# Output projection of a two-branch decoder layer by Strassen's scheme: 28 weight products of 512 columns in place of 32 per pair of blocks

## The chip, the cores and the metric

The kernel runs on one core of a Trainium2 chip. The metric is device time in microseconds (us), lower is better.

## The reference

One layer, on 4096 rows of 1024 float32 numbers:

```
proj  = x @ w_in                                  # 4096 x 1024 @ 1024 x 2832
out_a = sliding_window_attention(q_a, k_a, v_a, sinks) * silu(g_a)      # 512 wide
o_b   = gla_chunked(q_b * 64**-0.5, k_b, v_b, log_sigmoid(gate) / 16)
out_b = rmsnorm(o_b) * norm_w * silu(g_b)                               # 512 wide
mix   = concat(out_a, out_b) @ w_out              # 4096 x 1024 @ 1024 x 1024
x     = layer_norm(ALPHA * x + mix) * ln_g + ln_b
```

## The kernel before

The rows go in 32 blocks of 128. Every large product is made at close to float32 accuracy from fp32r parts: an operand is split into a rounded part h and the rest l, and three matmuls are summed (h with h, h with l, l with h). `project` (L130 to L137) issues them: TensorE has one 128 x 128 piece of the operand as its stationary side and 512 columns of the weights as its moving side. `split` (L97 to L105) makes the parts, an ACT cast at L100 and a subtraction at L105, mostly on DVE.

There are three stages, each a loop over the blocks. **Stage A** (0 to about 660 us) is the attention branch; its result goes to DRAM, one store per block. **Stage B** (to about 1356 us) projects q, k, v and the gate of the second branch (`bq`, `bv`, `bk`, `bg`), runs the gated linear attention, and in `b_store` (L679 to L688) transposes the block's result into PSUM (`to`, four TensorE transposes at L684), copies it with ACT and stores it to DRAM. The work of block n-1 stands between the projections of block n, so that TensorE has matmuls of one while DVE, ACT and POOL work at the other. **Stage C** (L738 to L780) is the output projection. Per block it loads both halves of the mix (`mr`) and the residual row (`xr`) from DRAM, splits the mix (`mh`, `ml`), and makes two halves of 512 columns (`py`), each 8 x 3 = 24 matmuls; DVE adds ALPHA times the residual as it reads the PSUM bank (L761) and takes the row statistics (L762, L763). Then comes the norm: a short chain on DVE and ACT gives `rs` (crs) and `nb`, ACT applies both (L777), POOL multiplies by the gain `lg` (L778), DVE adds the bias `lb` (L779), SP stores. The last block takes another way, on DVE alone (L771, L772). Before stage C the weights `w_out` are loaded and split by `load_group` (L108) in the last block of stage B.

What each engine does in which order is chosen by the framework's scheduler, which places instructions by priority (the order of the program, shifted by tc.high_priority) as it thinks they become ready; on the chip each engine then runs its list strictly in order. All transfers of this kernel are started by the one SP queue, also in order: a store whose data aren't ready holds up the loads listed behind it. A tile of a pool with `bufs=2` exists twice, and a third request waits for the first to come free. PSUM tags have two banks each.

Of the kernel before, what the change touches and what calls it, by code (L numbers as in the profile page):

```python
# [19 lines left out]
P = 128  # L20
# [30 lines left out]
def layer_kernel(  # L51
# [56 lines left out]
    def load_group(wr, src, c0, n, slot, width, early=False):  # L108
        hs, ls = [], []
        for k in range(NK):  # L110
            raw = wr.tile([P, 512], F32, tag="wraw", name=f"wraw{slot}_{k}")
            sp.dma_start(raw[:, :n], src[k, :, c0 : c0 + n])
            h = wp.tile([P, width], F32R, tag=f"wh{slot}_{k}", name=f"wh{slot}_{k}")
            l = wp.tile([P, width], F32R, tag=f"wl{slot}_{k}", name=f"wl{slot}_{k}")
# [15 lines left out]
    def project(dst, x, wg, n, k0=0, k1=NK):  # L130

        hs, ls = wg
        for k in range(k0, k1):
            a, b = x[0][:, k, :], x[1][:, k, :]
            pe.matmul(dst[:, :n], a, hs[k][:, :n], start=(k == 0), stop=False)  # L135
            pe.matmul(dst[:, :n], a, ls[k][:, :n], start=False, stop=False)  # L136
            pe.matmul(dst[:, :n], b, hs[k][:, :n], start=False, stop=(k == NK - 1))  # L137


    with ExitStack() as pa:  # L140
# [9 lines left out]
        wkv = load_group(wr, w_a, 512, 256, 1, 272, True)  # L150
# [189 lines left out]
        def a_out(n, pn, sg):  # L340
# [58 lines left out]
            sp.dma_start(mixd[n][0].rearrange("p a s -> p (a s)"), att)  # L399
# [5 lines left out]
        for n in range(NB):  # L405
# [19 lines left out]
            if n == NB - 2:  # L425
                wb["q"] = load_group(wr, w_b, 0, 272, 1, 272)
            if n == 2:
                wb["k"] = load_group(wr, w_b, 272, 256, 3, 256)
# [27 lines left out]
    def log_(dst, src, **kw):  # L456
        after(act.activation(dst, src, AF.Ln, **kw).ins, table.ins)


    with ExitStack() as pb:  # L460
        wr = pb.enter_context(tc.tile_pool(name="wrb", bufs=3))
# [47 lines left out]
        def b_sums(n):  # L509
# [6 lines left out]
            r0 = f1.tile([P, 256], F32, tag="r0", name=f"r0{n}")  # L516
# [14 lines left out]
            qp = f1.tile([P, 256], F32, tag="qp", name=f"qp{n}")  # L531
            pool.tensor_tensor(qp, B[n]["q"], ee, ALU.mult)  # L532
            B[n]["qp"] = qp
# [21 lines left out]
        def b_k(n, pk):  # L555
            kp = f1.tile([P, 256], F32, tag="kp", name=f"kp{n}")
            dve.tensor_tensor(kp, pk[:, :256], B[n]["ff"], ALU.mult)
            B[n]["kp"] = kp
# [63 lines left out]
        def b_gate(n, pg):  # L622
            gs = b1.tile([P, 512], F32, tag="gs", name=f"gs{n}")
            gw = b2.tile([P, 4, P], F32, tag="gw", name=f"gw{n}")
# [14 lines left out]
        def b_out(n):  # L639
# [31 lines left out]
            og = b1.tile([P, 512], F32, tag="og", name=f"og{n}")  # L671
# [7 lines left out]
        def b_store(n):  # L679
            og = B[n]["og"]  # L680
            to = bank("tp", f"to{n}")
            for h in range(4):
                hs = slice(h * P, (h + 1) * P)
                pe.transpose(to[:, hs], og[:, hs], ident)  # L684
            mb = b1.tile([P, 512], F32, tag="mb", name=f"mb{n}")
            act.copy(mb, to)
            sp.dma_start(mixd[n][1].rearrange("p a s -> p (a s)"), mb)
            B[n].clear() if n + 1 >= NB else None  # L688

        wo = [None, None]  # L690
        for n in range(NB):
# [4 lines left out]
            project(pq, x, wb["q"], 272, 0, 4)  # L696
# [3 lines left out]
            project(pq, x, wb["q"], 272, 4, NK)  # L700
# [17 lines left out]
            project(pk, x, wb["k"], 256)  # L718
            pg = bank("c", f"bg{n}")
            project(pg, x, wb["g"], 512, 0, 2)  # L720
            b_sums(n)
            b_k(n, pk)
# [5 lines left out]
            b_gate(n, pg)  # L728
            if last:
                wo[1] = load_group(wr, w_o, 512, 512, 2, 512)  # L730
# [7 lines left out]
    with ExitStack() as pcx:  # L738
        c1 = pcx.enter_context(tc.tile_pool(name="c1", bufs=1))
        c2 = pcx.enter_context(tc.tile_pool(name="c2", bufs=2))  # L740
        lg = c1.tile([P, D], F32, tag="lg", name="lg")
# [3 lines left out]
        for n in range(NB):  # L745
            raw = xp.tile([P, NK, P], F32, tag="xraw", name=f"mr{n}")
            sp.dma_start(raw[:, :4, :], mixd[n][0])
            sp.dma_start(raw[:, 4:, :], mixd[n][1])
            xr = c2.tile([P, D], F32, tag="xr", name=f"xr{n}")
            sp.dma_start(xr, xn[n * P : (n + 1) * P, :])  # L750
            mh = xp.tile([P, NK, P], F32R, tag="xh", name=f"mh{n}")
            ml = xp.tile([P, NK, P], F32R, tag="xl", name=f"ml{n}")
            split(mh, ml, raw, act, dve)
            y = c2.tile([P, D], F32, tag="y", name=f"y{n}")
            st = c2.tile([P, 2, 6], F32, tag="st", name=f"cst{n}")
            mv = c2.tile([P, 2], F32, tag="mv", name=f"mv{n}")
            for i in range(2):
                s = slice(512 * i, 512 * i + 512)
                py = bank(("pj", "tp")[n % 2], f"py{n}_{i}")
                project(py, (mh, ml), wo[i], 512)  # L760
                dve.scalar_tensor_tensor(y[:, s], xr[:, s], ALPHA, py, ALU.mult, ALU.add)  # L761
                dve.bn_stats(st[:, i, :], y[:, s])  # L762
            dve.bn_aggr(mv, st.rearrange("p a b -> p (a b)"))  # L763
            rs = c2.tile([P, 1], F32, tag="rs", name=f"crs{n}")
            nt = c2.tile([P, 1], F32, tag="nt", name=f"cnt{n}")
            rsqrt_eps(act, dve, log_, mv[:, 1:2], rs, nt, 1.0)
            rows = slice(n * P, (n + 1) * P)
            if n == NB - 1:
                for i in range(2):
                    s = slice(512 * i, 512 * i + 512)  # L770
                    dve.scalar_tensor_tensor(y[:, s], y[:, s], mv[:, 0:1], lg[:, s], ALU.subtract, ALU.mult)  # L771
                    dve.scalar_tensor_tensor(y[:, s], y[:, s], rs, lb[:, s], ALU.mult, ALU.add)  # L772
                    sp.dma_start(out[rows, s], y[:, s])
                break
            nb_ = c2.tile([P, 1], F32, tag="nb", name=f"nb{n}")
            dve.scalar_tensor_tensor(nb_, mv[:, 0:1], -1.0, rs, ALU.mult, ALU.mult)
            act.activation(y, y, AF.Identity, bias=nb_, scale=rs)  # L777
            pool.tensor_tensor(y, y, lg, ALU.mult)  # L778
            dve.tensor_tensor(y, y, lb, ALU.add)  # L779
            sp.dma_start(out[rows, :], y)  # L780
# [82 lines left out]
```

## Time and profile before

| | |
|---|---|
| median of 3 runs | 1724.26 us (1723.18 to 1724.8) |
| the profiled execution | 1724.99 us, span 1723.3 us, mean granted TensorE clock 0.996 |
| TensorE (PE) busy | 1691.6 us, 98% of the span |
| VectorE (DVE) busy | 1122.5 us, 65% |
| ScalarE (ACT) busy | 774.2 us, 45% |
| GpSimd (POOL) busy | 498.2 us, 29% |
| transfers | 119.68 MB, mean 69 GB/s; about 145 GB/s in stage C |

Engines run beside each other, so shares don't add up to 100%. PE is TensorE's matmul side, PEld its weight load, SPq the SP queue. A matmul of 512 columns shows as 0.39 us in the trace, but successive ones overlap: what counts is the distance from one start to the next. A name as `y<-y,lg` is output and inputs of an instruction, L778 the line of the kernel.

### The profile page before, as it was taken

Reading aid. Unit: us, or ns where it says so; the run is one execution under the profiler, and the core shown is the slowest. Engines: PE = TensorE matmul, PEld = TensorE weight load, DVE = VectorE, ACT = ScalarE, POOL = GpSimd, SP = SyncE. Lnnn points to the kernel's source line nnn. Section 1 sums busy time; section 2 is a strip of 40 time slices with the busy share of each in tenths; the row PEclk is TensorE's granted clock in tenths of the full one; section 3 lists DMA queues with packets and bytes.
Section 4 is the critical chain, followed back from the end, with each engine's and each line's share of the span. In section 5 each row is a group of like instructions: output and inputs, shape, how many; then the busy total and the mean of one; then the engine's idle time right before and its main releaser. Section 6 shows DMA issues by size and latency. Waiting matters only on the chain.

```text
span 1723.3 us, 26109 instructions
## 1 busy us (share of the span) xinstructions
PE 1691.6 (98%) x9466; PEld 1444.3 (84%) x9466; DVE 1122.5 (65%) x2547; ACT 774.2 (45%) x2064; POOL 498.2 (29%) x634
## 2 busy tenths in 40 slices
PE   7999999999999999999999999999999899999998
PEld 5788888888888887888888888888888788888886
DVE  6877777777777786666666666666665655555555
ACT  5444434444444455555555555555555522222221
POOL 3333322333222355222222222222222422222221
PEclk9999999999999999999999999999999899999999
DMA  6211111111111132111111111111111444444442
GB/s 197 80 38 37 37 46 47 37 38 38 37 53 40 37 102 79 50 38 38 38 38 38 38 38 38 38 38 38 38 37 38 153 146 143 142 144 146 147 147 86
DMA packets 65525, 119.68 MB, mean 69 GB/s; under 512 B 22642, under 2 KB 26100, under 8 KB 65396
## 3 DMA queue, kind: packets, MB, share of 16 engines
q1 hardware_dynamic: 65396, 118.01, 21.2%
q8 instruction: 74, 1.21, 0.3%
q14 instruction: 55, 0.45, 0.1%
HBM read 84.37 MB, written 33.62 MB: 68 GB/s over the span
## 4 chain that ended last, share of the span: by engine, by line
PE 58%; DVE 1%; ACT 1%; issue 0%; DMA 0%; POOL 0%; DVEq 0%; POOLq 0%; ACTq 0%
PE py L135 7%; PE py L137 7%; PE py L136 7%; PE bg L135 3%; PE bg L137 3%; PE bg L136 3%; PE bv L135 3%; PE bv L136 3%; PE bv L137 3%; PE bq L135 2%; PE bq L136 2%; PE bq L137 2%; PE bk L137 2%; PE bk L136 2%; PE bk L135 2%; PE to L684 1%
## 5 line engine op out<-in xcount | busy, mean ns | idle before, releaser
L361 POOL TENSOR_SCALAR_AFFINE_SELECT p<-hl 128x512 fp32r<-128x512 f32 x256 | 165.6, 682 | 382.7 <-ACT hl L355 348.8
L135 PE MATMUL py<-wh,mh 128*128 128x512 f32 x512 | 200.3, 391 | 0.0
L136 PE MATMUL py<-wl,mh 128*128 128x512 f32 x512 | 200.1, 391 | 0.0
L137 PE MATMUL py<-wh,ml 128*128 128x512 f32 x512 | 200.1, 391 | 0.0
L330 ACT ACTIVATE pr<-psc,ngm 128x128 f32<-128x128 f32 x256 | 90.7, 367 | 193.8 <-PE psc L311 138.1
L778 POOL TENSOR_TENSOR y<-y,lg 128x1024 f32<-128x1024 f32 x31 | 74.2, 2394 | 269.0 <-ACT y L777 253.5
L532 POOL TENSOR_TENSOR qp<-bqs,ee 128x256 f32<-128x256 f32 x32 | 23.6, 738 | 337.3 <-ACT ee L529 323.9
L137 PEld LDWEIGHTS py<-wh,ml 128*128 128x128 f32 x512 | 96.7, 189 | 20.3
L135 PEld LDWEIGHTS py<-wh,mh 128*128 128x128 f32 x512 | 96.7, 189 | 20.0
L136 PEld LDWEIGHTS py<-wl,mh 128*128 128x128 f32 x512 | 96.7, 189 | 19.8
L135 PE MATMUL pq<-wh,xh 128*128 128x512 f32 x256 | 105.0, 410 | 7.4 <-ACT wh L100 6.3
L135 PE MATMUL pg<-wh,xh 128*128 128x512 f32 x256 | 110.5, 433 | 0.1
L135 PE MATMUL bg<-wh,xh 128*128 128x512 f32 x256 | 107.0, 418 | 0.0
L137 PE MATMUL pq<-wh,xl 128*128 128x512 f32 x256 | 102.6, 401 | 1.2 <-DVE xl L105 1.2
L135 PE MATMUL bv<-wh,xh 128*128 128x512 f32 x256 | 103.5, 404 | 0.0
L100 ACT CAST mh<-mr 128x1024 fp32r<-128x1024 f32 x32 | 33.7, 1054 | 154.2 <-PE py L136 154.2
L105 DVE TENSOR_TENSOR xl<-xraw,xh 128x512 fp32r<-128x512 f32 x128 | 94.7, 760 | 11.6 <-ACT xh L100 5.2
L136 PE MATMUL pq<-wl,xh 128*128 128x512 f32 x256 | 102.1, 399 | 0.1
L136 PE MATMUL pg<-wl,xh 128*128 128x512 f32 x256 | 100.6, 393 | 1.3 <-POOL wl L105 1.0
L137 PE MATMUL pg<-wh,xl 128*128 128x512 f32 x256 | 101.0, 395 | 0.0
L136 PE MATMUL bv<-wl,xh 128*128 128x512 f32 x256 | 100.9, 394 | 0.0
L137 PE MATMUL bg<-wh,xl 128*128 128x512 f32 x256 | 100.7, 393 | 0.0
(221 smaller groups left out, 4907.1 us busy)
## 6 DMA issues: line engine op xcount, KB each, us to landing
xraw<-in_xt_dram SPq DMA_DIRECT2D x64, 512.0 KB
mr<-mx SPq DMA_DIRECT2D x64, 256.0 KB
xr<-in_xn_dram SPq DMA_DIRECT2D x32, 512.0 KB
out_dram<-y SPq DMA_DIRECT2D x31, 512.0 KB
mx<-att SPq DMA_DIRECT2D x32, 256.0 KB
mx<-mb SPq DMA_DIRECT2D x32, 256.0 KB
wraw<-in_w_a_dram SPq DMA_DIRECT2D x16, 256.0 KB
wraw<-in_w_b_dram SPq DMA_DIRECT2D x16, 256.0 KB
```

The source lines that it names most:

```text
L100: act.copy(hdst, src)
L105: leng.tensor_tensor(ldst, src, hdst, ALU.subtract)
L135: pe.matmul(dst[:, :n], a, hs[k][:, :n], start=(k == 0), stop=False)
L136: pe.matmul(dst[:, :n], a, ls[k][:, :n], start=False, stop=False)
L137: pe.matmul(dst[:, :n], b, hs[k][:, :n], start=False, stop=(k == NK - 1))
L330: act.activation(pr[:, i], sc[i], AF.Exp, bias=ngm[:, h : h + 1], scale=0.125, accum_out=den[:, h : h + 1])
L361: pool.affine_select(o, hl[:, i], [[0, 4], [sg_, P]], ALU.is_gt if b else ALU.is_ge, 0.0, base=0, channel_multiplier=-sg_,)
L532: pool.tensor_tensor(qp, B[n]["q"], ee, ALU.mult)
L684: pe.transpose(to[:, hs], og[:, hs], ident)
L778: pool.tensor_tensor(y, y, lg, ALU.mult)
```

## The change

A **pair** is two successive blocks, even and odd, and each block's mix has two halves of 512 numbers (branch A, branch B): call these four 128 x 512 operands a11, a12 (even) and a21, a22 (odd). The weights are four 512 x 512 quarters. Strassen's scheme in Winograd's form makes the four 128 x 512 results of a pair with 7 products where the direct way has 8; each product takes one sum or difference of operands and one of weights, and results are sums of products. A product is 4 x 3 = 12 matmuls of 512 columns, so a pair takes 84 in place of 96, and the 16 pairs 1344 in place of 1536.

- **Operand sums.** In stage B `b_rows` loads the pair's branch A halves back, and the new `b_store` makes the sums on DVE, one with an even block besides a difference, three with an odd one, reading the transposed block `to` from PSUM. Seven operands per pair are stored to DRAM (`opd`).
- **Weight sums.** `w_prepare` loads w_out's quarters in 8 chunks, makes 7 combinations of each, splits them (7 ACT casts, 7 DVE subtractions and 4 DVE differences of 128 x 256 per chunk) and stores h and l parts to DRAM (`wod`, 28 tiles of 512 KB, 14.7 MB). The program asks for two steps a block with `tc.high_priority(offset=-300)`. `w_fetch` loads the 28 tiles at the end of stage B and the start of stage C, six products' weights into the places of stage B's weights and one into new tiles.
- **Stage C.** Seven steps of 12 matmuls (`STEPS`). Bank a takes t0, t2, t4 and t6, each summed on top of what is there, bank b t1 and t5, bank c t3. After each step DVE adds the bank into the result tile `y` (`READS`; L962, L964). A bank is read between its steps, so that the first matmul of t2, t4, t6 and t5 waits until DVE has read the bank. `y` is loaded from the residual rows by SP. Pairs 0 and 1 go step by step in turn, the others one after the other.
- **The norm** (`normed`) runs in the steps of the next pair. POOL multiplies by `lg` in halves (L914); `lb` is added in halves on POOL for the even block, on DVE (L918) for the odd one. The store is put behind the latest operand load on SP.
- **Room.** The k weights ride with the q weights in one load of 528 columns; some tiles of stage B share places, `gw` has one buffer in place of two.

```diff
+        def b_store(n):
...
             mb = b1.tile([P, 512], F32, tag="mb", name=f"mb{n}")
-            act.copy(mb, to)
-            sp.dma_start(mixd[n][1].rearrange("p a s -> p (a s)"), mb)
+            act.copy(mb, tof)
+            sp.dma_start(opd[p][4 + odd], mb)
+            a11, a21 = B[n - odd]["at"]
+            if not odd:
+                dve.tensor_tensor(a11, a11, a21, ALU.subtract)
+                sp.dma_start(opd[p][2], a11)
+                ax = b1.tile([P, 512], F32, tag="ax", name=f"ax{p}")
+                dve.tensor_tensor(ax, tof, a11, ALU.add)
+                B[n]["ax"] = ax
+                return
+            ax = B[n - 1]["ax"]
+            dve.tensor_tensor(a21, tof, a21, ALU.add)
+            sp.dma_start(opd[p][3], a21)
+            dve.tensor_tensor(a11, tof, a11, ALU.subtract)
+            sp.dma_start(opd[p][1], a11)
+            dve.tensor_tensor(ax, ax, tof, ALU.subtract)
+            sp.dma_start(opd[p][6], ax)
...
+            def part(i, src):
+                w = b2.tile([P, 2, 256], F32R, tag="wo", name=f"wop{i}_{k}{c}")
+                split(w[:, 0], w[:, 1], src, act, dve)
+                sp.dma_start(wod[i][k][:, :, 256 * c : 256 * c + 256], w.bitcast(F32))
...
-            if last:
-                wo[0] = load_group(wr, w_o, 0, 512, 0, 512)
+            with tc.high_priority(offset=-300):
+                next(prep, None)
...
+        def split_op(w, i):
+            h, l = w[i]
+            act.copy(h, l.bitcast(F32))
+            dve.tensor_tensor(l, l.bitcast(F32), h, ALU.subtract)
...
+        def normed(n, y, st, late, tail):
...
+            act.activation(y, y, AF.Identity, bias=nb_, scale=r2)
+            yield
+            for s in (LO, HI):
+                pool.tensor_tensor(y[:, s], y[:, s], lg[:, s], ALU.mult)
+            if late is dve:
+                yield
+            for s in (LO, HI):
+                late.tensor_tensor(y[:, s], y[:, s], lb[:, s], ALU.add)
+            yield
+            after(sp.dma_start(out[rows, :], y).ins, latest[0])
...
+        STEPS = (("a", 0, False), ("b", 3, False), ("a", 1, True), ("c", 4, False), ("a", 2, True), ("b", 6, True), ("a", 5, True))
+        READS = ((0, 0, True), (1, 1, True), (0, 1, True), (0, 0, False), (1, 1, False), (0, 1, False), (1, 0, True))
...
+            product(b[x], ops[p], op, more)
+            i, half, first = READS[t]
+            y, s = ys[p][i], (LO, HI)[half]
+            if first:
+                dve.scalar_tensor_tensor(y[:, s], y[:, s], ALPHA, b[x], ALU.mult, ALU.add)
+            else:
+                dve.tensor_tensor(y[:, s], y[:, s], b[x], ALU.add)
+            if t in (3, 4, 5, 6):
+                dve.bn_stats(st[i][:, half, :], y[:, s])
+            run_later()
```

How the orders move is seen at three places. On DVE in stage C of the kernel before, around blocks 15 and 16 (`py` is the bank, `ml` the split's rest): the bias add of the block before (L779) stands behind a bank's read (L761) and ahead of its statistics.

```order
L761 SCALAR_TENSOR_TENSOR y15_17273<-xr15_17267,py15_0_17276 128x512
L779 TENSOR_TENSOR y14_17192<-y14_17192,lb_16046 128x1024
L762 BN_STATS cst15_17274<-y15_17273 128x6
L761 SCALAR_TENSOR_TENSOR y15_17273<-xr15_17267,py15_1_17303 128x512
L762 BN_STATS cst15_17274<-y15_17273 128x6
L105 TENSOR_TENSOR ml17_17432<-mr17_17426,mh17_17431 128x1024
```

In the changed kernel, the same engine at the start of pair 8 (blocks 16 and 17; pa8, pb8, pc8 are its banks; ol5_9, oa10 and oc10 operand tiles being split):

```order
L962 SCALAR_TENSOR_TENSOR y16_17820<-y16_17820,pa8_17886 128x512
L866 TENSOR_TENSOR ol5_9_17882<-ol5_9_17882,oh5_9_17881 128x512
L899 TENSOR_SCALAR cnt15_17875<-crs15_17874 128x1
L900 TENSOR_SCALAR cnt15_17875<-cnt15_17875,mv15_17873 128x1
L901 TENSOR_SCALAR cr215_17876<-cnt15_17875,crs15_17874 128x1
L910 TENSOR_SCALAR nb15_17911<-mv15_17873,cr215_17876 128x1
L962 SCALAR_TENSOR_TENSOR y17_17822<-y17_17822,pb8_17887 128x512
L918 TENSOR_TENSOR y15_17648<-y15_17648,lb_16497 128x512 x2
L962 SCALAR_TENSOR_TENSOR y16_17820<-y16_17820,pa8_17886 128x512
L866 TENSOR_TENSOR oa10_17949<-oa10_17949,ob10_17950 128x512 x2
L964 TENSOR_TENSOR y16_17820<-y16_17820,pc8_17888 128x512
```

The two bias adds of block 15 (L918) now stand ahead of the read of bank a after t2 (the second L962 of y16), which t4 on TensorE waits for. It is so in the pairs 4, 5, 7, 8, 10, 11, 13, 14 and 15; in 3, 6, 9 and 12 they stand behind it. And on POOL, what comes ahead of those adds, with two halves in each row:

```order
L914 TENSOR_TENSOR y14_17646<-y14_17646,lg_16496 128x512 x2
L918 TENSOR_TENSOR y14_17646<-y14_17646,lb_16497 128x512 x2
L914 TENSOR_TENSOR y15_17648<-y15_17648,lg_16496 128x512 x2
L914 TENSOR_TENSOR y16_17820<-y16_17820,lg_16496 128x512 x2
L918 TENSOR_TENSOR y16_17820<-y16_17820,lb_16497 128x512 x2
```

Block 15's gain is now behind four half operations for block 14, where each block had one whole operation before. Last, the SP queue at the turn from stage B to stage C (op15_5, _3, _1 and _6 are stores of the last pair's operands, wo2 weights of product 2, y0 to y3 the residual rows, ol4 operands of product 4):

```order
L792 DMA wo2_0_16460<-wod2_0_205 128x1024
L694 DMA op15_5_179<-mb31_16409 128x512
L706 DMA op15_3_177<-a21_30_16050 128x512
L708 DMA op15_1_175<-a11_30_16048 128x512
L710 DMA op15_6_180<-ax15_16261 128x512
L792 DMA wo2_1_16462<-wod2_1_206 128x1024
L792 DMA wo2_2_16464<-wod2_2_207 128x1024
L882 DMA y0_16432<-in_xn_dram 128x1024
L882 DMA y1_16434<-in_xn_dram 128x1024
L771 DMA ol4_0_16437<-op0_4_73 128x512
```

In the kernel before the residual rows of the first two blocks (L750, `xr0`, `xr1`) were ahead of the last store of stage B (L687); now they are behind four.

## Rows read from the trace of the kernel before

**Rows 1.** The chain that ended last, first shares, from the page.
```profile
PE 58%; DVE 1%; ACT 1%; issue 0%; DMA 0%; POOL 0%; DVEq 0%; POOLq 0%; ACTq 0%
```

**Rows 2.** Windows of stages B and C, busy us and counts (header first).
```profile
core 0: us, PE busy (x) PEld busy (x) DVE busy (x) ACT busy (x) POOL busy (x), PEclk, DMA share, GB/s
900.00:1100.00 200.00, 200.00 (x1246) 176.43 (x1245) 122.58 (x291) 109.86 (x270) 52.06 (x66) 1.00 0.13 39
1400.00:1500.00 100.00, 100.00 (x443) 82.81 (x442) 55.45 (x111) 24.83 (x37) 21.54 (x9) 1.00 0.42 144
```

**Rows 3.** Timeline, PE, from stage B to C: start, us, idle before and releaser.
```profile
1347.25 0.38 PE L513 MATMUL pc<-lal,cum 128*128 128x256 f32 x1 [0.30 <-DVE lal L105]
1349.53 1.26 PE L684 MATMUL to<-cs,og 128*128 128x128 f32 x4 [1.89 <-DVE og L674]
...
1358.36 0.40 PE L135 MATMUL py<-wh,mh 128*128 128x512 f32 x1
...
1364.56 0.66 PE L651 MATMUL bo<-bvv,al 128*128 128x128 f32 x4 [0.86 <-DVE al L105]
...
1366.84 0.79 PE L658 MATMUL bo<-sbh,bth 128*128 128x256 f32 x2 [1.33 <-ACT sbh L550]
...
1375.18 0.38 PE L684 MATMUL to<-cs,og 128*128 128x128 f32 x2
```

**Rows 4.** Windows within that turn; the last three columns are clock, DMA share, GB/s.
```profile
1348.00:1352.00 4.00, 2.47 (x8) 1.94 (x9) 3.07 (x7) 1.74 (x4) 0.99 (x1) 0.69 0.63 191
1368.00:1371.00 3.00, 3.00 (x10) 2.61 (x10) 1.00 (x3) 1.38 (x3) 0.00 (x0) 0.50 0.88 355
1371.00:1374.00 3.00, 3.00 (x9) 2.32 (x9) 2.27 (x10) 0.41 (x2) 0.00 (x0) 0.60 0.62 254
```

**Rows 5.** Groups of instructions, 1400 to 1700 us: count | busy us, mean ns | idle before, releaser.
```profile
L761 DVE SCALAR_TENSOR_TENSOR y<-xr,py 128x512 f32<-128x512 f32 x56 | 38.5, 687 | 70.6 <-PE py L137 70.6
L762 DVE BATCH_NORM_STATS2 cst<-y 128x6 f32<-128x512 f32 x55 | 38.0, 690 | 1.0
L105 DVE TENSOR_TENSOR ml<-mr,mh 128x1024 fp32r<-128x1024 f32 x28 | 33.8, 1206 | 0.0
L779 DVE TENSOR_TENSOR y<-y,lb 128x1024 f32<-128x1024 f32 x27 | 33.1, 1226 | 47.2 <-POOL y L778 47.2
L777 ACT ACTIVATE y<-y,nb,crs 128x1024 f32<-128x1024 f32 x28 | 34.8, 1244 | 22.7 <-DVE nb L776 22.7
L778 POOL TENSOR_TENSOR y<-y,lg 128x1024 f32<-128x1024 f32 x28 | 67.0, 2394 | 237.6 <-ACT y L777 237.6
```

**Rows 6.** Groups in stage B, 900 to 1300 us, operations of a half row's size.
```profile
L636 POOL TENSOR_TENSOR gw<-gw,gs 128x512 f32<-128x512 f32 x19 | 24.7, 1298 | 54.9 <-ACT r L481 54.9
L105 DVE TENSOR_TENSOR bvv<-bv,bvv 128x512 fp32r<-128x512 f32 x19 | 13.1, 691 | 0.0
L612 DVE TENSOR_TENSOR tot<-pu,st 64x256 f32<-64x256 f32 x38 | 15.8, 417 | 0.3
```

**Rows 7.** Timeline of one norm in stage C.
```profile
1695.89 0.20 DVE L763 BATCH_NORM_AGGREGATE mv<-cst 128x2 f32<-128x12 f32 x1
1696.12 0.15 DVE L785 TENSOR_SCALAR mv<-mv 128x1 f32<-128x1 f32 x1
...
1697.36 0.16 DVE L776 SCALAR_TENSOR_TENSOR nb<-mv,crs 128x1 f32<-128x1 f32 x1
1697.56 1.24 ACT L777 ACTIVATE y<-y,nb,crs 128x1024 f32<-128x1024 f32 x1 [0.81 <-DVE nb L776]
...
1698.88 2.39 POOL L778 TENSOR_TENSOR y<-y,lg 128x1024 f32<-128x1024 f32 x1 [8.49 <-ACT y L777]
```

**Rows 8.** Timeline at 205 us, POOL and DVE with operands in SBUF.
```profile
205.05 1.61 POOL L361 TENSOR_SCALAR_AFFINE_SELECT p<-hl 128x512 fp32r<-128x512 f32 x2 [12.17 <-ACT hl L355]
205.50 0.67 DVE L243 TENSOR_TENSOR qk<-ra,rb 128x80 f32<-128x80 f32 x1
```

**Rows 9.** All executions of that DVE line: min/median/max ns.
```profile
L243 DVE TENSOR_TENSOR qk<-ra,rb x32: 225/670/674, 30.2 to 631.5; 128x80 f32<-128x80 f32 x32
```

**Rows 10.** Timeline, the end.
```profile
1714.76 0.39 PE L137 MATMUL py<-wh,ml 128*128 128x512 f32 x1
...
1715.19 0.69 DVE L761 SCALAR_TENSOR_TENSOR y<-xr,py 128x512 f32<-128x512 f32 x1 [1.45 <-PE py L137]
...
1719.50 0.99 SPq L773 DMA_DIRECT2D out_dram<-y  x2
```

More of the change, by code (lines that the diff above doesn't have):

```diff
@@ L699, in layer_kernel @@
                 b_state(n - 1)
[L700 removed]
+            project(pq, x, wb["qk"], 272, 4, NK)
             b_qr(n, pq)
@@ L721, in layer_kernel @@
             b_sums(n)
+            if last:
+                w_fetch(0)
+            if n == NB - 3:
+                for _ in prep:
+                    pass
             b_k(n, pk)
@@ L728, in layer_kernel @@
             b_gate(n, pg)
+            with tc.high_priority(offset=-300):
+                next(prep, None)
             if last:
-                wo[1] = load_group(wr, w_o, 512, 512, 2, 512)
+                ops = [op_places(p) for p in range(2)]
+                w_fetch(3)
+                w_fetch(1)
+            b_rows(n)
         b_attn(NB - 1)
@@ new lines, in product @@
+        def product(dst, w, i, more=False):
+            h_, l_ = w[i]
+            for k in range(4):
+                h, l = wo[i][k][:, 0, :512], wo[i][k][:, 1, :512]
+                a, b = h_[:, k * P : (k + 1) * P], l_[:, k * P : (k + 1) * P]
+                pe.matmul(dst, a, h, start=(not more and k == 0), stop=False, skip_group_check=more)
+                pe.matmul(dst, a, l, start=False, stop=False, skip_group_check=more)
+                pe.matmul(dst, b, h, start=False, stop=(k == 3), skip_group_check=more)
@@ L741, in layer_kernel @@
+        ORDER = (0, 3, 1, 4, 2, 6, 5)
+        ys = []
+        for i in (4, 2, 6, 5):
+            if i in (4, 2):
+                ys.append(load_rows(len(ys)))
+            for p in range(2):
+                op_more(p, ops[p], (i,))
+            w_fetch(i, c1 if i == 5 else None)
         lg = c1.tile([P, D], F32, tag="lg", name="lg")
@@ L744, in layer_kernel @@
         sp.dma_start(lb, ln_b.partition_broadcast(P))
[L745 to L780, printed above, removed]
@@ new lines, in layer_kernel, with run_later @@
+        for i in ORDER:
+            for p in range(2):
+                split_op(ops[p], i)
+        pairs, later = NB // 2, []
+        def run_later():
+            for g in list(later):
+                if next(g, 0) == 0:
+                    later.remove(g)
+        STEPS = (("a", 0, False), ("b", 3, False), ("a", 1, True), ("c", 4, False), ("a", 2, True), ("b", 6, True), ("a", 5, True))
+        READS = ((0, 0, True), (1, 1, True), (0, 1, True), (0, 0, False), (1, 1, False), (0, 1, False), (1, 0, True))
@@ new lines, in layer_kernel, with step @@
+        state = {}
+        def step(p, t):
+            if t == 0:
+                b = {x: bank(g, f"p{x}{p}") for x, g in (("a", "pj"), ("b", "c"), ("c", "d"))}
+                st = [c2.tile([P, 2, 6], F32, tag=f"st{i}", name=f"cst{2 * p + i}") for i in range(2)]
+                state[p] = b, st
+            b, st = state[p]
+            x, op, more = STEPS[t]
+            product(b[x], ops[p], op, more)
[3 more added lines that the diff above has]
+                dve.scalar_tensor_tensor(y[:, s], y[:, s], ALPHA, b[x], ALU.mult, ALU.add)
+            else:
+                dve.tensor_tensor(y[:, s], y[:, s], b[x], ALU.add)
+            if t in (3, 4, 5, 6):
+                dve.bn_stats(st[i][:, half, :], y[:, s])
+            run_later()
+            if t in (5, 6):
+                g = normed(2 * p + i, y, st[i], (pool, dve)[i], p == pairs - 1 and i == 1)
+                next(g)
+                later.append(g)
@@ L783, in rsqrt_eps @@
+        while later:
+            run_later()
 def rsqrt_eps(act, dve, log_, ms, rs, nt, scale):
```

176 lines of the change are left out of this document (147 added, 29 removed).

## The prediction

> **What bounds the kernel now.** I read the chain of waits first: 58% of the span lies on PE and next to nothing on any other engine [rows 1]. Then the windows: in stages B and C PE is busy for the whole of the window, at a clock of 1.00, while DVE is busy 61% in B and 55% in C, and POOL 22% in C [rows 2]. So TensorE is the limit, and a matmul less is worth its full distance. In stage C 443 start in 100 us, one each 0.2257 us [rows 2]. The other place to look at is the turn from B to C, where PE isn't dense: block 30's transposes waited 1.89 us and `bo` 0.86 and 1.33 [rows 3], and behind such waits the granted clock was 0.50 to 0.69 [rows 4]. The third is the norm of stage C: its long operations (ACT 1244 ns, POOL 2394, DVE 1226) now have much slack, seen as POOL's 237.6 us of idle time [rows 5]. The forecast turns on whether they still have it.
>
> The sum is made against the profiled execution, 1724.99 us, which is 0.7 above the median of 1724.26; I take 0.7 off at the end. A difference of 0.2%, 3.4 us, is about what a measurement can tell from none.
>
> **What the change costs and brings, part by part.**
>
> (1) Matmuls: 32 blocks x 48 = 1536 become 16 pairs x 84 = 1344. 192 x 0.2257 = **-43.3 us**. This much is sure, as far as PE stays dense.
>
> (2) The splits of `w_out` leave the last block of stage B. They stand on ACT, DVE and POOL beside the waits there, 1.89 us and a slow clock behind it [rows 3, 4]. I take **-3**; between 0 (the new sums of `b_store` take the place) and -4.6, what that block loses now: the 1.89, 0.30 and the slow stretch of 1350 to 1353, by the windows some 2.4.
>
> (3) The start of stage C. What it pays now: stage C's matmuls take 1536 x 0.2257 = 346.7, the rest of block 31's own matmuls some 4; from the end of its gate projection at 1356.3 to the last matmul's end at 1715.15 it is 358.9, so 8.2 are lost. What it will pay: block 31's transposes come 16.8 us behind the first output matmul [rows 3], set by a chain over DVE and ACT that the change leaves alone. Ahead of them PE now has 33 matmuls (7.4 us), some 4 us of `bo` and the waits of 2.2 us [rows 3]: it waits about 2.6. Behind them 16 matmuls (3.6) until t2 of pair 0, which needs bank a read, and the read needs `y0`. That load stands on SP behind four stores, of which the last needs three DVE sums behind the transposes (0.6 for ACT's copy, else 3 x 0.69 by the size's row, [rows 5, 6]), and behind 1 MB of weights. With its own 0.5 MB at 355 GB/s [rows 4] it lands 4 to 5 us later than it is issued; PE waits about 6. With the first two waits some 4 (0.86 and 1.33 and a late `y2`), and two spells at half the clock, 3 us as now, it is about 16. **+8**, between +2 and +20. Behind this the transfers must keep up: 14 MB are wanted until product 5 of pair 0, some 42 us after room for them comes free; at 355 GB/s that is 40 us, so they just do.
>
> (4) The steady pairs. A pair takes PE 84 x 0.2257 = 18.96 us. DVE has 7 reads, 4 statistics, 7 splits and 2 halves of bias, 20 x about 0.69 [rows 5, 6], with small ones some 15.7: it fits. The queue fits too: 3.9 MB per pair is 207 GB/s, under the 355. But the norm's chain is new in its order. Count from the first matmul of a pair: the even block's last sums are read behind t5, but `nb` stands on DVE behind the read of t6 and comes at about 1.6 to 1.9; ACT takes 1.24 [rows 5, 7], so POOL starts at 3.1. It then has six half operations ahead of the odd block's bias add: gain twice and bias twice for the even block, gain twice for the odd one, each 1.20 (half of 2394) to 1.30 [rows 5, 6], so 7.2 to 7.8: it ends at 10.3 to 10.9. In nine pairs the two bias adds (1.23, [rows 5]) stand on DVE ahead of the read of t2 (0.69 and some 0.3 of hand-over): bank a comes free at 12.5 to 13.1. PE wants it for t4 at 4 x 2.71 = 10.8. So PE waits 1.7 to 2.3 in these pairs, at a clock that stays: waits of 1.3 and 0.9 had a slow clock only with others close by [rows 3, 4]. I take 2.2: 9 x 2.2 = **+20**. Bounds: 0, if the chain comes 2 us sooner, and 43, which rival 2 works out. Where the adds stand behind that read (pairs 3, 6, 9, 12) they delay only reads that have a step's time left, and cost nothing; if this cover fails too, 4 x 1.2.
>
> What could lengthen the chain is seen at 205 us: a small DVE operation with two inputs in SBUF began while POOL ran and took 0.67 us [rows 8], where the shortest of its kind took 0.225 [rows 9]; so one waited for the other. In stage C the splits and bias adds on DVE have two inputs in SBUF, and POOL now runs 8 us of 19. Each meeting costs one of the two up to an operation, 0.65 or 1.2; I have put one half of the first into the 2.2. The Trainium skill (SBUF — State Buffer, Who interferes with whom) says that a DVE instruction with two SBUF inputs and a GpSimd instruction that reads SBUF hold a shared port pair by turns, for the whole instruction. The row agrees; by that rule every meeting is a full wait, which is rival 2's sum.
>
> (5) The end. Now 8.15 us from the last matmul's end to the end of the span [rows 10]. Block 31 keeps its own short way, but block 30 has POOL's four halves (4 x 1.25) behind ACT, and its store stands on SP ahead of block 31's: about 11.8. **+3.6**, between 0 and 6.
>
> (6) Weight sums in stage B. 8 x (7 + 4) DVE operations of 128 x 256 at 0.417 [rows 6] are 37 us, and as many casts on ACT. The order has them all in the first seven blocks, some 15 per block: 6.3 us on top of DVE's 13.2 (61% of a block's 21.56), with operand sums of 1.4 about 20.7. That fits in the mean, but the chain of the gated attention passes over DVE several times per block, and the h and l tiles have two buffers that each wait for a store. **+3**, between 0 and +8. Operand sums in the later blocks (2.1 on DVE in odd ones, 8.4 idle) and four small loads and stores a block, at 39 GB/s [rows 2], are hidden in the idle time of DVE and the queue; without it each would cost its 0.7. The k weights' one load and the shared tiles: 0.
>
> Sum: -43.3 - 3 + 8 + 20 + 3.6 + 3 = -11.7. 1724.99 - 11.7 = 1713.3, as a median 1712.6: **1713 us**, on its own 1702 to 1722.
>
> **Rivals.**
>
> *1. The reads come in time.* If the scheduler's order is as good as it thinks, POOL's halves overlap with ACT's end, or `nb` comes before t6's read, and the 2 us at stake per pair vanish. For it: the excess is only 2 us on a chain of 13, and POOL's half operation has been seen only whole. Against it: POOL's row gives no reason for a half being under 1.2. Without the 20: 1693 us, with a start of +5 some 1690. Chance 0.22.
>
> *2. The norm's chain decides, and it gets slower than before.* One mechanism: bank a's read behind the bias adds, behind POOL. If each pair meets the wait of rows 8 once on POOL (0.65) and once on DVE (0.6 to 1.3), the wait is 3.4 in five pairs, 4 in the four (4, 7, 10, 13) where `nb` stands behind one more split, and a wait of this length was followed by a slow clock (the 1.89 one, [rows 3, 4]), 1.2 each: 5 x 4.6 + 4 x 5.2 = 43.8 in place of 20. 1713 + 23.8 = 1736 us. It decides from where waits sum to more than what the other terms bring, 31.7, or 3.5 per pair of nine. For it: the row at 205 us, and the skill's rule. Against it: a PE that waits gives DVE time to catch up, and the splits can fall into POOL's idle time. Chance 0.28.
>
> *3. The start runs out of transfers.* At 254 GB/s, the other rate seen [rows 4], the 14 MB take 56 us in place of 42 and PE waits some 13 more in pairs 0 to 2: 1726 us. For it: stores and loads share one queue in order, so one late store holds all. Against it: 355 was reached a moment before. Chance 0.10.
>
> That the change doesn't do what it says can be left out: the order has 192 matmuls fewer.
>
> **How the numbers follow.** Forecast 0.40, the rivals 0.22, 0.28 and 0.10. The range of 1686 to 1738 takes in rival 1 with a good start and most of rival 2, whose bad end (waits in all pairs) is left out. Faster by over 0.2% is under 1720.8: nearly all of the forecast (0.37), rival 1 (0.22) and a little of rival 3 (0.02): 0.61. Within 0.2% is up to 1727.7: the rest of the forecast, half of rival 3 and the low end of rival 2: 0.12. Slower: 0.27.
>
> **What would show it.** In the profile after: 0.2257 us per matmul in dense stretches; in stage C one wait of PE of 1.7 to 2.3 us before the first matmul of t4, put down to DVE's read, in nine of the pairs from 2 on and in none of 3, 6, 9, 12; POOL half operations of 1.2 to 1.3; a wait of some 6 us before t2 of pair 0 with the load of `y0` behind it; blocks 0 to 6 of stage B at most 0.5 us longer than the others. Wrong it is if PE stays dense in pairs 3 to 15 (rival 1), if those waits are over 3.5 with clocks of 0.5 to 0.7 between (rival 2), or if most waits of pairs 0 to 2 end with a transfer (rival 3).

## The result and the profile after

| | before | after |
|---|---|---|
| median | 1723.72 us (4 runs) | 1791.65 us (4 runs, 1789.25 to 1793.82) |
| profiled span | 1723.3 us | 1792.0 us |
| PE busy | 98% | 94% |
| granted clock, mean | 0.996 | 0.982 |

The changed kernel is slower by 3.9% (ratio 1.0393, 95% interval 1.0375 to 1.0411), though it has 192 matmuls fewer. The forecast was 1713, with a range up to 1738. Windows of the profile after, with the columns of [rows 2]:

```profile
710.00:840.00 130.00, 121.37 (x727) 103.58 (x726) 105.55 (x252) 76.70 (x201) 31.55 (x39) 1.00 0.58 186
900.00:1100.00 200.00, 196.31 (x1215) 172.33 (x1214) 133.36 (x304) 107.57 (x263) 50.01 (x64) 1.00 0.23 76
1500.00:1600.00 100.00, 86.04 (x348) 68.57 (x347) 65.72 (x135) 31.37 (x55) 35.15 (x27) 0.93 0.48 158
1600.00:1700.00 100.00, 87.25 (x363) 69.38 (x362) 65.84 (x130) 29.18 (x53) 35.36 (x28) 0.97 0.51 167
```

PE is dense in none of these windows. In stage C it starts 348 to 363 matmuls in 100 us, where it started 443 [rows 2], and the clock is below 1; stage B has lost too, most in its first blocks. By places, from the starts of the transposes `to` (block 0: 702.83, was 698.85; block 30: 1378.66, was 1349.53 [rows 3]) and the last matmul's end (1778.08, was 1715.15 [rows 10]):

| stretch | before | after | difference |
|---|---|---|---|
| to block 0's transposes | 698.85 | 702.83 | +4.0 |
| from there to block 30's | 650.7 | 675.8 | +25.2 |
| to the last matmul's end | 365.6 | 399.4 | +33.8 |
| to the end of the span | 8.15 | 13.9 | +5.8 |

The sum is 68.7 before rounding, the difference of the spans. In the third stretch 43.3 us of matmuls went, so its losses grew by 77. Up to 1442.67, where pair 2 begins, it loses 64.0 - 2 x 18.96 = 26.1, where the whole of stage C lost 18.9 before: +7. The rest, 70 us, is in pairs 2 to 15: they take 24.0 us each in place of 18.96. PE's waits there (who waited for whom, in total, times, longest):

```profile
PE pa L874 <- DVE y L962: 28.2, 12, 4.6
PE pa L874 <- DVE y L964: 8.8, 7, 3.2
PE pa L874 <- ACT ob L865: 7.5, 3, 4.6
PE pc L876 <- DVE ol L866: 1.0, 1, 1.0
PE pa L876 <- DVE oa L866: 0.6, 1, 0.6
```

These are 46 us, and all the large ones stand ahead of a first matmul on bank a, that is, behind a bank's read on DVE (where ACT is named, the cast of pair 2's first operand is one; the others came at the same moment as a read). The other 24 us are the clock and the start of each step after a wait: by the granted clock some 16 of them are matmuls at half the pace, an estimate, and a pair with one wait of 1.84 takes 21.25 where 18.96 + 1.84 would be 20.8. Chosen rows of the timeline at pair 10, which begins at 1635.55, show one such wait and what is behind it:

```profile
1635.85 1.25 ACT L865 CAST oh<-ol 128x512 fp32r<-128x512 f32 x2 [5.08 <-DMA ol<-op]
1636.50 0.69 DVE L866 TENSOR_TENSOR ol<-ol,oh 128x512 fp32r<-128x512 f32 x1 [3.18 <-ACT oh L865]
1644.18 2.55 POOL L914 TENSOR_TENSOR y<-y,lg 128x512 f32<-128x512 f32 x2 [16.39 <-ACT y L911]
1645.10 0.68 DVE L962 SCALAR_TENSOR_TENSOR y<-y,pb 128x512 f32<-128x512 f32 x1
1646.69 2.54 POOL L918 TENSOR_TENSOR y<-y,lb 128x512 f32<-128x512 f32 x2
1649.19 2.48 POOL L914 TENSOR_TENSOR y<-y,lg 128x512 f32<-128x512 f32 x2
1649.26 0.34 SPq L920 DMA_DIRECT2D out_dram<-y  x1
1649.65 0.43 SPq L771 DMA_DIRECT2D oa<-op  x1
1650.49 2.33 DVE L918 TENSOR_TENSOR y<-y,lb 128x512 f32<-128x512 f32 x2 [4.71 <-POOL y L914]
1652.74 0.67 DVE L962 SCALAR_TENSOR_TENSOR y<-y,pa 128x512 f32<-128x512 f32 x1
1653.34 0.62 ACT L865 CAST ob<-oa 128x512 fp32r<-128x512 f32 x1 [6.32 <-DMA oa<-op]
1653.57 0.76 PE L874 MATMUL pa<-wo,oh 128*128 128x512 f32 x1 [4.62 <-DVE y L962]
1654.13 0.63 PE L875 MATMUL pa<-wo,oh 128*128 128x512 f32 x1
```

The first three rows are the start of it: ACT's cast waits 5.08 us for an operand's load, the split on DVE 3.18 for the cast, and `nb` and POOL's first gain, which come behind, are late: POOL begins 8.6 us into the pair. DVE then stands 4.71 us ahead of the bias adds until POOL's gain is done, the adds take 2.33, then comes the read of t2, and PE goes on 4.62 late, at 0.43 from one start to the next: the granted clock of 1653 to 1659 was 0.50, the lower of the two levels. Beside it SP starts the load of the next operand (L771) right behind a store (L920) that waited for POOL, and ACT's cast of that operand waited 6.32 for the load.

### The profile page after: what moved, and what is told of

Read it like the earlier page. It is cut to its first block, busy times and chain, and to the rows that moved or that the text cites. A ratio compares the mean times of both kernels' runs of the same rounds, so it can differ in the third digit from the quotient of the medians.

```text
span 1792.0 us, 26780 instructions
## 1 busy us (share of the span) xinstructions
PE 1680.7 (94%) x9274; PEld 1417.7 (79%) x9274; DVE 1266.0 (71%) x2830; ACT 810.2 (45%) x2176; POOL 539.8 (30%) x685
## 5 line engine op out<-in xcount | busy, mean ns | idle before, releaser
L914 POOL TENSOR_TENSOR y<-y,lg 128x512 f32<-128x512 f32 x62 | 84.6, 1386 | 268.5 <-ACT y L911 222.1
L143 PE MATMUL pg<-w,xh 128*128 128x512 f32 x256 | 110.7, 434 | 0.3 <-DVE vv L259 0.3
L143 PE MATMUL pq<-w,xh 128*128 128x512 f32 x256 | 103.9, 406 | 6.6 <-ACT w L107 6.3
L143 PE MATMUL bg<-w,xh 128*128 128x512 f32 x256 | 106.0, 414 | 0.0
L143 PE MATMUL bv<-w,xh 128*128 128x512 f32 x256 | 103.2, 403 | 0.0
L145 PE MATMUL pq<-w,xl 128*128 128x512 f32 x256 | 101.5, 397 | 1.0 <-DVE xl L112 1.0
L144 PE MATMUL pg<-w,xh 128*128 128x512 f32 x256 | 101.0, 395 | 1.2 <-POOL w L112 1.0
L145 PE MATMUL pg<-w,xl 128*128 128x512 f32 x256 | 101.6, 397 | 0.0
L144 PE MATMUL pq<-w,xh 128*128 128x512 f32 x256 | 101.1, 395 | 0.1
L144 PE MATMUL bv<-w,xh 128*128 128x512 f32 x256 | 100.8, 394 | 0.0
L145 PE MATMUL bv<-w,xl 128*128 128x512 f32 x256 | 100.8, 394 | 0.0
L145 PE MATMUL bg<-w,xl 128*128 128x512 f32 x256 | 100.2, 392 | 0.0
L144 PE MATMUL bg<-w,xh 128*128 128x512 f32 x256 | 100.2, 391 | 0.0
L384 PE MATMUL po<-p,vv 128*128 128x512 f32 x252 | 79.3, 417 | 4.1 <-POOL p L369 3.6
```

Of the source, the lines that this page charges most:

```text
L143: pe.matmul(dst[:, :n], a, hs[k][:, c], start=(k == 0), stop=False)
L144: pe.matmul(dst[:, :n], a, ls[k][:, c], start=False, stop=False)
L145: pe.matmul(dst[:, :n], b, hs[k][:, c], start=False, stop=(k == NK - 1))
L384: pe.matmul(po, vvs[n - b][:, g, :], parts.pop((g, b, i)).rearrange("p h s -> p (h s)"), start=(b == 0 and i == 0), stop=(b == 1 and i == 1),)
L914: pool.tensor_tensor(y[:, s], y[:, s], lg[:, s], ALU.mult)
```

## The experiments

Each run is the changed kernel with an edit, shown shortened and with comments added; `after(i, j)` puts instruction i behind j in the order. Times are single executions where no interval stands, beside runs of the kernel before of 1722 to 1725 us on the same chip.

**Bias adds behind the read of t3 (e1).**

```diff
+            if late is dve:
+                yield          # one step more
             for s in (LO, HI):
-                late.tensor_tensor(y[:, s], y[:, s], lb[:, s], ALU.add)
+                i = late.tensor_tensor(y[:, s], y[:, s], lb[:, s], ALU.add).ins
+                if late is dve:
+                    after(i, read[0])      # the latest bank read on DVE
```

> Edit: the two bias adds of the odd block on DVE are put behind the read of t3 in place of ahead of the read of t2; nothing else. If the order on DVE (bank a's read behind a bias add that waits for POOL) makes the waits of PE ahead of t4, the ten waits of 1.1 to 4.8 us there (28 us) go, and with them the slow clock behind the four long ones (12): about 1752 us. If DVE is simply too full, the waits move to t2 or t6 and less than 10 us come back. If the operand loads set the pace, nothing changes, and most waits end with a DMA.

1771.76 us, 20 less where 40 were expected. All waits ahead of t4 but one (1.14) are gone, but 23.0 us in ten waits now stand ahead of t6: half of what was hoped for moved. Behind them is a split of a later pair's operand that stands on DVE ahead of the reads of t3 and t4 and waits for its load.

**Both bias adds on POOL (e2).**

```diff
-                g = normed(2 * p + i, y, st[i], (pool, dve)[i], ...)
+                g = normed(2 * p + i, y, st[i], (pool, pool)[i], ...)
```

> Edit: the odd block's bias add goes to POOL as the even block's does, so DVE waits for POOL nowhere and has 1.2 us less per pair, while POOL has 8 half operations of 1.25 to 1.4, some 11 of 19 us. If the waits come from DVE standing behind POOL: as the first run, about 1750 us. If the shared access of POOL and DVE to SBUF costs as much as the order, the splits on DVE meet more of POOL's operations, and it is 10 us or more above the first run. If result tiles come free too late, waits that end with a load of y appear at t0, and it is above 1770.

1803.95 us, 12 more, though DVE waits for POOL nowhere. Chosen rows of the timeline of pair 8 say why:

```profile
1609.21 0.34 SPq L920 DMA_DIRECT2D out_dram<-y  x1
1609.60 0.42 SPq L771 DMA_DIRECT2D oa<-op  x1
1612.90 0.62 ACT L865 CAST ob<-oa 128x512 fp32r<-128x512 f32 x1 [6.38 <-DMA oa<-op]
1614.20 0.34 SPq L920 DMA_DIRECT2D out_dram<-y  x1
1614.64 0.37 SPq L771 DMA_DIRECT2D oc<-op  x1
1618.09 0.62 ACT L865 CAST oc<-oc 128x512 fp32r<-128x512 f32 x1 [4.57 <-DMA oc<-op]
1618.74 0.69 DVE L866 TENSOR_TENSOR oc<-oc 128x512 fp32r<-128x512 f32 x1 [3.41 <-ACT oc L865]
1619.35 0.68 DVE L964 TENSOR_TENSOR y<-y,pa 128x512 f32<-128x512 f32 x1
1620.18 0.76 PE L874 MATMUL pa<-wo,oh 128*128 128x512 f32 x1 [6.26 <-DVE y L964]
```

The store waits on SP until POOL is done, the operand's load behind it starts late and takes 3.5 us, ACT's cast waits for it, DVE's subtraction for the cast, the bank's read stands behind the subtraction, and PE waits 6.26. From 1480 to 1740 us SP's stores waited 94.7 us for POOL (22 times), in the changed kernel 53.8 (11 times). None of the three cases that were written down had this: POOL holds PE through two paths, DVE's adds and SP's stores. The time alone would fit the second case (it is 32 us above e1), and the splits of `oa` did get longer beside POOL, 1105 ns on the mean in place of 682 (1480 to 1715 us); f2, below, tells the two apart.

**No gain and no bias (f4).**

```diff
             for s in (LO, HI):
-                pool.tensor_tensor(y[:, s], y[:, s], lg[:, s], ALU.mult)
+                pass
...
-                late.tensor_tensor(y[:, s], y[:, s], lb[:, s], ALU.add)
+                pass
```

> Edit: the changed kernel without the multiplication by lg and the addition of lb in all blocks but the last, so this part of the norm is left out; POOL has nothing to do in stage C, the stores wait for ACT alone. If POOL's chain is the root (through DVE's adds, and through the stores that hold SP's queue and with it the loads and the splits), nearly all of the 71 us of pairs 2 to 15 go: 1720 to 1735. If the splits wait for loads for another reason, or DVE is too full, some 30 us of waits stay ahead of t2 and t6: 1750 to 1765.

1736.68 us, 55 less, just outside the first case: three quarters of the 70 hang on the gain and the bias. The edit takes away POOL's chain with both its paths, but also 2.4 us of bias adds a pair on DVE and all meetings of the two engines, so by itself it doesn't say which of these counts. Some 10 us of waits, none over 1.4, are left, most at t2 and t6.

**Splits in their step (f1), and with it the bias adds (f2).**

```diff
-            act.copy(h, l.bitcast(F32))
-            dve.tensor_tensor(l, l.bitcast(F32), h, ALU.subtract)
+            i = act.copy(h, l.bitcast(F32)).ins
+            j = dve.tensor_tensor(l, l.bitcast(F32), h, ALU.subtract).ins
+            if read[0] is not None:
+                after(i, read[0])
+                after(j, read[0])
```

> Edit: the splits of the next pair's operands (ACT cast, DVE subtraction) are tied behind the bank read of the step that asks for them, where the scheduler had them up to a pair sooner; the bias adds then stand behind the read of t2 in all pairs. If splits that wait on DVE for loads which stand on SP behind stores make the waits ahead of t2 and t6 (the first run left 30 us of waits there), these go and only waits on POOL's chain are left, now ahead of t6: pairs of 20 to 22 us, 1745 to 1760. If POOL's chain alone counts, the waits only change their place: 1775 or more. If the transfers themselves are too slow, waits that end with a cast of a late load appear at t0: 1780 or more.

> Edit: the run before and the first run's edit together: splits in their step and bias adds behind the read of t3. If the order on DVE is the whole cause in stage C (reads behind adds that wait for POOL, and behind splits that wait for loads), pairs 3 to 15 take 19 to 19.5 us in place of 24.0 on average and the time is about 1725. If DVE is too full in itself (15.7 us of 18.96 and what it loses to POOL at the shared access), 15 us or more of waits stay: 1740 or more.

1754.78 us, as expected, and 1740.96. With f1 each pair from 4 to 14 takes 20.4 us and has one wait of 0.9, ahead of t6; with f2, 19.6 and a wait of at most 0.2. PE's waits in pairs 2 to 15 of f2 sum to 5.1 us, where the changed kernel has 46. So the order of DVE's and ACT's lists is the cause in stage C: nothing was taken away, only put later. Rows of f2 (1450 to 1720 us; L917 is the gain) show that it isn't by itself what POOL and DVE cost each other, nor that DVE is too full:

```profile
L917 POOL TENSOR_TENSOR y<-y,lg 128x512 f32<-128x512 f32 x56 | 83.0, 1503 | 145.3 <-ACT y L914 91.8 <-ACT crs L463 53.5
L866 DVE TENSOR_TENSOR oa<-oa,ob 128x512 fp32r<-128x512 f32 x26 | 36.7, 1413 | 14.0 <-ACT ob L865 13.9
```

POOL's halves and these splits take longer than in the changed kernel (1370 and 718 ns, 1450 to 1770 us), SP's stores still wait 59.3 us for POOL (12 times, 1480 to 1715 us), and PE hardly notices. The expected 1725 for f2 was missed by 16; the time falls into the second case of the expectation, whose sign, 15 us of waits, is absent. Some 13 of the 16 can be placed: pairs 2 and 3, which begin while the start's loads are late, still took 23.8 and 21.2 (6 us over 19.5), the others some 0.35 each over what was expected (4), and the part ahead of stage C took 3 us more in this execution. A queue of their own for the stores was not tried.

**Weight sums two steps a block (e3).**

```diff
-            with tc.high_priority(offset=-300):
-                next(prep, None)
+            next(prep, None)
...
-                split(w[:, 0], w[:, 1], src, act, dve)
+                held(act.copy(w[:, 0], src))       # after() this block's row sums on DVE
+                held(dve.tensor_tensor(w[:, 1], src, w[:, 0], ALU.subtract))
```

> Edit: the operations of the weight sums are tied to the block that asks for them, two steps a block, in place of all in the first seven blocks. The first six blocks of stage B took 143.8 us in place of 129.6. If the crowd there (DVE and ACT nearly full, two tiles that wait for their stores) makes this, spreading gives most of the 14 back: about 1779 us. If each of these operations costs its time wherever it stands, the later blocks get 0.5 longer each and the total stays at 1790 within 3.

1759.01 us, 33 less, more than twice what was expected. All but four blocks of stage B (the first, one in the middle and the last two) now take 21.4 to 21.5, against 21.56 before the change: the first six gave back 14.8, and every second one of the later blocks, which had taken 22.81, gave back its excess too. For these the order had changed along: `dd`, the small difference that the decay of the state needs, takes 0.15 us in every block and stands ahead of the gate's operations on DVE, and the difference a11 - a21 no longer stands between it and the state's decay.

**The difference moved (e4).**

```diff
-                dve.tensor_tensor(a11, a11, a21, ALU.subtract)
+                after(dve.tensor_tensor(a11, a11, a21, ALU.subtract).ins, carry[0])
```

> Edit: the difference a11 - a21 stands on DVE behind the row sums of the next block, where DVE idles 0.65 us for ACT, in place of ahead of the attention weights and the state decay of the odd block. Every second block of stage B took 22.8 us in place of 21.5. If that operation (0.68) and the small difference dd that meets POOL's operation (0.93 in place of 0.15) make it, about half of 1.28 x 12 goes with the first: 8 us less, 1783. If the three sums behind the transposes make it, nothing changes. If both go (dd comes sooner as well), 1776.

1777.15 us, 14.5 less. The long blocks, every second one from the seventh on, fell from 22.81 to 22.22, some 6 us in all, and the first six gave some 6 as well. So the number came near the third case, where both operations go, but only the first did: `dd` still takes 0.92 us in the long blocks. The timeline of the changed kernel has the rest, in a long block and (last row) a short one:

```profile
1187.93 1.30 POOL L641 TENSOR_TENSOR gw<-gw,gs 128x512 f32<-128x512 f32 x1 [2.82 <-ACT gs L634]
1188.32 0.93 DVE L546 TENSOR_TENSOR dd<-sm,sm 128x2 f32<-128x2 f32 x1
1189.17 0.68 DVE L698 TENSOR_TENSOR a<-a,a 128x512 f32<-128x512 f32 x1
1193.04 0.38 PE L664 MATMUL bo<-sbl,bth 128*128 128x256 f32 x1 [0.73 <-POOL sbl L556]
...
1164.99 0.15 DVE L546 TENSOR_TENSOR dd<-sm,sm 128x2 f32<-128x2 f32 x1
```

`dd` takes 0.93 when it meets POOL's operation and ends with it, 0.15 when it does not, and the operand difference L698 stands behind it: 0.78 + 0.68 in front of the state's decay, which `bo` on PE waits for.

**All places (f3), the rows' place (h1), and both (g4).** f3 is f2 with e3, with the first four loads of y on ACT's queue, and with both blocks of the last pair normed on DVE. h1 opens the pool of y first:

```diff
+        c4 = pcx.enter_context(tc.tile_pool(name="c4", bufs=5))
         c1 = pcx.enter_context(tc.tile_pool(name="c1", bufs=1))
         c2 = pcx.enter_context(tc.tile_pool(name="c2", bufs=2))
-        c4 = pcx.enter_context(tc.tile_pool(name="c4", bufs=5))
```

> Edit: the run before, and with it: weight sums two steps a block (as in e3_prep_spread), the first four residual rows loaded through ACT's queue in place of SP's, behind the last operand stores, and both blocks of the last pair normed on DVE in place of POOL. By the parts, from 1792: 66 less in stage C, 33 in stage B, 6 at the start of stage C if the load behind the stores makes the 8.3 us wait before t2 of pair 0, 4 to 5 at the end (13.9 us behind the last matmul now): about 1683, 2.3% under the kernel before. If the terms overlap (a wait closed in one place opens in the next), 1700 to 1715. If the causes are others, over 1724.

> Edit: the changed kernel with the pool of the result tiles y opened ahead of the other two pools of stage C, so that the first two of them lie in memory that stage B has left sooner, and their loads stand ahead of the last four operand stores on SP. In the run with all edits the loads went through ACT's queue and still began only 2.9 us behind the last store's issue, so the place in memory, not the queue, is the suspect. If so, the wait of 8.3 us ahead of t2 of pair 0 falls to under 3 and the slow clock behind it shortens: 1782 to 1787. If the operand and weight loads behind (product 4) are what is late, the wait moves to t3 and the time stays within 3 us of 1792.

> Edit: the run with all edits, with the first rows by their place in memory (as in the run beside it) in place of ACT's queue, and the bank reads on DVE tied to stand in the order of the steps (pair 2 waited 6.0 us at t5 since its read of t1 stood behind two bias adds). From 1705.5: 5 to 6 less at the start of stage C, 6 to 8 less in pair 2 with its clock: about 1692. If the start is bound by transfers, 1698. If the order of reads makes DVE wait for a late row elsewhere, 1705 or more.

f3: 1705.52 us, ratio to the kernel before 0.9893 (0.9876 to 0.9909); 1683 had been expected, and 1700 to 1715 if the terms overlap, as they did. The end fell from 13.9 to 10.4 us. The start didn't gain: the wait ahead of t2 of pair 0 was 8.99. Chosen rows of the changed kernel, and below them those of f3:

```profile
1402.52 0.39 SPq L710 DMA_DIRECT2D op<-ax  x1
1405.46 0.81 SPq L882 DMA_DIRECT2D y<-in_xn_dram  x2
1410.49 0.69 DVE L962 SCALAR_TENSOR_TENSOR y<-y,pa 128x512 f32<-128x512 f32 x1 [8.50 <-DMA y<-in_xn_dram]
1411.23 0.79 PE L874 MATMUL pa<-wo,oc 128*128 128x512 f32 x1 [8.34 <-DVE y L962]
```

```profile
1371.02 0.32 SPq L712 DMA_DIRECT2D op<-ax  x1
1373.93 0.38 ACTq L890 DMA_DIRECT2D y<-in_xn_dram  x1
1380.89 0.79 PE L882 MATMUL pa<-wo,oc 128*128 128x512 f32 x1 [8.99 <-DVE y L973]
```

On a queue of its own the load begins 2.91 us behind the last store's issue, as on SP (2.94). With the other place in memory (h1) the first rows load before the stores and that wait is 3.7, so it was the place that y had to wait for, not the queue. But h1 as a whole gained nothing that can be told: its 1790.11 lies within the runs of the changed kernel, as waits of 3.4 and 5.6 appeared in pair 2, where the operands are late in their turn. g4, which is f3 with h1's place in place of ACT's queue and with the bank reads tied to the order of the steps: 1702.27 us, ratio 0.9867 (0.9851 to 0.9884); a version that beats both kernels, by 1.3% and 5%. It was expected at 1692: pairs 0 to 3, with block 31's last matmuls among them, take 100 us where the pairs alone would be 76 dense, with waits of 3.5, 3.4 and 4.0 and the clock behind them. Whether the transfers alone bound this start was not tried.

## Why the prediction was wrong

**(1)** held: f2's and g4's steady pairs run at 19.6 us, 18.96 and a few tenths at the turns.

**(2) and (3)**, the turn, came out nearly as summed: -3 + 8 = +5 forecast; measured are -2.6 in the block that ends with block 30's transposes (25.24 us before, 22.63 now) and +7 behind them, so some +4.5. For (2) the mechanism held: the transposes, which had waited 1.89 us, wait for nothing now.

```profile
1378.66 0.60 PE L689 MATMUL to<-cs,om 128*128 128x128 f32 x4
```

That the sum of (3) came so near is partly luck: the wait of 2.6 ahead of block 31's transposes (3.2 by the terms given there) didn't come, and the one at t2 of pair 0 was 8.3 where 6 was said. The reason given was half wrong: not SP's order alone, but the memory that y shares with stage B's last operands.

**(4)** failed. Its number, +20, was +70. The chain itself was read rightly: in pairs 5, 8, 11 and 14 POOL begins 3.11 us into the pair (3.1 was forecast) and the wait ahead of t4 is 1.84 (1.7 to 2.3 was forecast), with POOL's halves at 1.37 and 1.33 us. The first row is pair 11, which begins at 1664.57; the others are groups, 1450 to 1770 us:

```profile
1667.68 3.00 POOL L914 TENSOR_TENSOR y<-y,lg 128x512 f32<-128x512 f32 x2 [16.00 <-ACT y L911]
L914 POOL TENSOR_TENSOR y<-y,lg 128x512 f32<-128x512 f32 x56 | 75.5, 1370 | 209.3 <-ACT y L911 209.3
L918 POOL TENSOR_TENSOR y<-y,lb 128x512 f32<-128x512 f32 x27 | 35.3, 1327 | 0.0
L918 DVE TENSOR_TENSOR y<-y,lb 128x512 f32<-128x512 f32 x30 | 34.8, 1197 | 47.9 <-POOL y L914 47.9
L865 ACT CAST oh<-ol 128x512 fp32r<-128x512 f32 x56 | 33.9, 614 | 60.3 <-DMA ol<-op 56.4 <-PE pb L875 3.2 <-PE pa L876 0.4
```

The step that failed is the start of that chain: `nb` "at about 1.6 to 1.9" was counted for all nine pairs, and the operand loads were put at nothing. In pairs 4, 7, 10 and 13 `nb` comes at 5.1 to 6.6 and POOL begins at 6.7 to 8.6 us, since DVE stands ahead of them in a split that waits for its load; the wait is 4.5 to 4.6, not 2.2, and the granted clock behind it falls to 0.50. Rival 2 had such pairs, at 4 and 1.2, and it was 4.6 and some 3. In pairs 3, 6, 9 and 12 the bias adds behind the read were to "cost nothing"; PE waits 3.2, 1.2, 1.3 and 1.3 ahead of t6 there. And "The queue fits too" looked at bytes only: the store on SP waits for the bias add, the loads behind it wait with it, and the splits that the scheduler had put ahead of the bank reads wait for the loads. That is the ACT row above, 56.4 us of waiting for loads, and e2's rows show it without DVE's waits for POOL. DVE's spare time (15.7 of 18.96 used) was taken as cover, though it is spent standing in front of such a wait. Rival 2 named the right mechanism and side, but at 1736 it was too cheap for want of the second path.

What POOL and DVE cost each other was seen in [rows 8, 9] and set too low: a bias half on DVE takes 1197 ns beside POOL, where a whole one took 1226 in the kernel before, behind POOL's operation [rows 5]; with POOL idle (f4) the splits take 680, in the changed kernel 790. By itself it doesn't make the 70, though, as f2 shows. By the Trainium skill (SBUF — State Buffer, Who interferes with whom) a DVE instruction with two SBUF inputs contends with a GpSimd instruction that reads SBUF, over a port pair that is an exclusive lock. The trace agrees: `dd` takes 0.93 us in place of 0.15 when it meets POOL's operation, and ends with it.

**(5)** was +3.6, measured +5.8. Of the 2.2 more, 1.5 are POOL's four halves, 6.5 us in place of 5.0; they run beside DVE's operations for the last block, which take 1.2 a half where the kernel before had 0.74. That the two meet is the likely reason; no run took it apart:

```profile
1780.13 2.41 DVE L905 SCALAR_TENSOR_TENSOR y<-y,mv,lg 128x512 f32<-128x512 f32 x2
1780.53 3.13 POOL L914 TENSOR_TENSOR y<-y,lg 128x512 f32<-128x512 f32 x2 [12.79 <-ACT y L911]
1783.62 3.38 POOL L918 TENSOR_TENSOR y<-y,lb 128x512 f32<-128x512 f32 x2
1787.02 0.33 SPq L920 DMA_DIRECT2D out_dram<-y  x1
```

**(6)** failed: +3 forecast, some +28 measured, the 25.2 of the table with the 2.6 that (2) brought back added. The first six blocks cost 14 (bound: 8), and e3 gave them back; that ACT and DVE serve the weight sums between links of the attention's chain is the reason argued here, not separated from the new order that came with e3. The operand sums that "are hidden in the idle time of DVE" cost some 1.25 in every second block from the seventh on, 14 in all: idle time in the sum says nothing of one 0.68 us operation in front of the decay. The load of 528 columns was set at 0, but by the first product of stage B (646.6 before, 649.0 now) 2.4 us are lost. The trace places the loss in the block of stage A where this load is split: up to there the changed kernel is 1.7 us ahead, behind it 2.4 late, and PE waits there for POOL, which makes splits of 528 columns beside its own work; no run took it apart.

```profile
633.96 1.09 PE L384 MATMUL po<-p,vv 128*128 128x512 f32 x2 [2.01 <-POOL p L369]
```

## What to carry to other kernels

Idle time of an engine covers an added instruction only where it stands: read from the order what is listed behind it on that engine and who waits for that, and do so for the DMA queue too, where one store that waits for a late engine holds every load behind it. A scheduler that puts preparatory work as early as it thinks possible lets that work wait in front of urgent reads; tying the splits and the bias adds to their steps (f2) took 51 us off the changed kernel without removing an instruction. A gain in matmuls is worth having only after the waits on PE have been counted bank by bank.

## What was not expected of the hardware

DVE's bias half went from half of 1226 ns to 1197 and POOL's half of a multiplication from half of 2394 to 1370, with POOL busy only 35% and DVE 66% of the time: in the rows shown the long operation is the one that began second, `dd` behind POOL's L641 and the bias adds at 1650.49 behind POOL's L914. In pairs 4, 7, 10 and 13 a wait of 4.5 to 4.6 us on PE was followed by twelve matmuls at a granted clock of 0.50 to 0.52, one of 1.84 by none in the changed kernel, while in e3 and e4 some waits of 1.84 were followed by matmuls at 0.50 (0.63 over the twelve behind the one that ends at 1572.13 in e3). In e2 two waits of 2.78 us were followed by twelve matmuls at 1.00 and by twelve at 0.50. The length of the wait alone doesn't decide it; what else does stays open here. Opening a pool of tiles in another order let the first load of y go 4.1 us behind the first output matmul (g4), where it went 20.0 behind it in the changed kernel.
